# Mixer side chains resumed by an estimate of operand times instead of counted delays, on one Trainium2 core

## The chip, the core and the metric

The kernel runs on one core of one Trainium2 chip. The metric is the device time of one execution in microseconds (us). Names of engines are those of the profile: PE is TensorE's matmul queue, PEld its weight loads, DVE is VectorE, ACT is ScalarE, POOL is GpSimd, SP is SyncE, which issues nearly all DMAs here. Line numbers (L610) are those of the kernel before; where a line of the changed kernel is meant, the text says so.

## What is computed

One layer over 2048 tokens of width 1024, in fp32. The part that the change touches is the mixer:

```python
p = h @ w_in[layer]
gate_b, gate_c, h_conv, q, k, v, z, a, bt = jnp.split(p, split_at, axis=-1)
ya = gate_b * causal_depthwise_conv(gate_c * h_conv, conv_w_mix[layer])       # then a grouped rms_norm
q, k, v = silu(causal_depthwise_conv([q, k, v]))                               # q and k then L2-normalised
g_dec = -exp(a_log) * softplus(a + dt_bias)
o = chunked_gated_delta_rule(q, k, v, g_dec, beta)    # per chunk: decay matrix, triangular solve, state step
yb = rms_norm(o, g_dn_out[layer]) * silu(z)
x = x + gate_m * (concat([ya, yb]) @ w_out[layer])
```

Ahead of it stands a normalisation with modulation by `c`, behind it a gated feed-forward layer of hidden width 2816 and a final normalisation. Those are the same in both kernels.

## The kernel before

**Tiling.** The mixer works through four blocks of 512 tokens (b = 0 to 3). A block has 28 projections of 128 output columns (4 heads each of k, q, v and z, then 12 for the short convolution, in triples `cg`, `hc`, `gb`). A projection is 24 matmuls of 128x128 by 128x512: 8 slices of the inner dimension times three products of high and low halves (`whi`/`wlo` for weights, `hTh`/`hTl` for activations), since each fp32 operand is split into two fp32r parts. These are recorded by `dmm` (L122) into the PSUM tiles `pd` and are called dense matmuls below. Each strip of weights is loaded by SP, rounded on ACT (`whi`, L189) and its remainder taken on DVE (`wlo`, L191); up to three strips stand ready ahead. The block ends with the output projection, 2 x 96 dense matmuls. After the mixer comes the feed-forward part.

**Side chains.** Everything that is not a dense matmul is written as Python generators that record instructions and `yield`. `dmm` counts dense matmuls, and after each sixth it calls `tick`, which resumes every chain whose delay has run out; `yield n` means "resume after n ticks", that is after 6n dense matmuls. So the numbers behind `yield` and the delays of `spawn` decide where in each engine's instruction stream a chain's next piece stands. (The framework that records the program moves some instructions between engines' queues afterwards, so the true places are read from the built program.) All engines execute their own queue in order.

**The chains of a block, in the order in which they depend on each other:**

- `head_chain`, first part: `proj_ab` (L536) gives 16 rows per token block; they are copied, transposed (L629), and a softplus with a series is computed in small steps, 18 of them on POOL, down to `g` (L659). Then `yield 7`, three small matmuls (L670 to L672), an exponential `eg`, and per head the decay matrix `E` (L680 to L688).
- `head_chain`, second part, per head: k is transposed to tokens (L610) and scaled by `eg` into `kd` (L696); its norm `nk` (L697); k times k (L704), times `E` into `M` (L706, tile name `ym`), scaled on POOL (L707), masked on POOL (L710) and reduced on DVE into the head's part of `Dg` (L714).
- The inversion of the 32x32 diagonal blocks: `Dg` of all four heads goes to DRAM (`dm`) and comes back in another layout (`mq`, part of a tile named `yal`); then 31 steps of two DVE instructions (L736, L738) that depend on each other; the result goes to DRAM (`dx`) and comes back as `xc` (tile name `Dg`); POOL spreads it into `X` (L752, 32 instructions).
- `level_chain`, twice two heads: transposes of `X` on DVE (L768), a masked `M` called `Mm` (L770), matmuls L775 and L782, and then the half-size steps L790 to L804, which complete the inverse.
- `q_chain` (L817, L818), `v_chain` (L830), then `chunk_chain`, four chunks of 128 tokens in sequence through `state`, and per chunk `out_chain`, which gives the hi and lo halves that the output projection reads. `mix_chain` (L957 to L963) normalises the convolution branch into `yah` and `yal`.
- `second_norm` of the block before (L295 to L362) runs beside a block; its transposes are L360.

Small matmuls and transposes of all chains go to the PSUM tiles `pm`, four in rotation, so a chain's matmul can wait until an older user of its `pm` tile has been read. Scratch tiles in SBUF rotate too: `cv` (4), `lv` (6), `ch` (4).

Of the kernel before, what the change touches and what calls it, by code (L numbers as in the profile page):

```python
# [37 lines left out]
PRE = 3  # L38
HALF = 1024


def constants():
    i = np.arange(P)
    r, c = i[:, None], i[None, :]
    parts = [r == c, r <= c, r > c, r // 64 == c // 64]
    for b in LEVELS:
        parts.append((r // (2 * b) == c // (2 * b)) & (r % (2 * b) < b) & (c % (2 * b) >= b))
    parts.append(r // BASE == np.arange(NBASE)[None, :])
    return np.ascontiguousarray(np.concatenate(parts, axis=1).astype(np.float32))


@with_exitstack
def layer_kernel(ctx, tc, x, c, w_ada, b_ada, w_ada_final, b_ada_final, g_norm_mix, g_norm_ffn, g_norm_final,
# [49 lines left out]
    side, count = [], [0]  # L103
# [4 lines left out]
    def tick():  # L108
        for e in list(side):
            e[1] -= 1  # L110
            if e[1] <= 0:
                try:
                    e[1] = next(e[0]) or 1
                except StopIteration:
                    side.remove(e)

    def drain():
        while side:
            tick()
# [219 lines left out]
    def transpose_split(tiles, gcol, scol, hh, hl):  # L339
        for k in range(KD):  # L340
            scale_split(transpose_k(tiles, k), k, gcol, scol, hh, hl)
            yield 2
# [8 lines left out]
    def second_norm(b):  # L351
        for i in range(CH):
# [3 lines left out]
            yield 2  # L356
            for q in range(2):
                ps = misc_ps()
# [5 lines left out]
                yield 1  # L364
# [93 lines left out]
    with ExitStack() as actx:  # L458
# [117 lines left out]
        for b in range(NB):  # L576
            hh, hl = hT
            if b:
# [39 lines left out]
            def wait(key, n):  # L618
                while done[key] < n:
                    yield 1  # L620


            def head_chain(ps, b=b):
                abr = cv_tile([P, BLK])[:16, :]
                nc.vector.tensor_copy(abr, ps[:16, :])
                yield 1
                ps = misc_ps()
                for j in range(CH):
                    nc.tensor.transpose(ps[:, j * 16:(j + 1) * 16], abr[:, j * P:(j + 1) * P], ident[:16, :16])  # L629
                ab2 = ap_.tile([P, CH, 16], F32, name="ab2")  # L630
# [36 lines left out]
                yield 7  # L667
# [8 lines left out]
                for h in range(NH):  # L676
                    rgs = []
# [4 lines left out]
                    yield 3  # L682
                    ps = misc_ps()
                    for i, rg in enumerate(rgs):
                        mm(ps, strict_r, rg.rearrange("p j c -> p (j c)"), start=(i == 0), stop=(i == 1))
                    e = ap_.tile([P, CH, P], F32, name="E", bufs=4)
# [5 lines left out]
                for h in range(NH):  # L692
                    yield from wait("k", h + 1)
                    pk = to_tokens(kT[:, h, :])
# [13 lines left out]
                    Ms.append(M)  # L708
                    md = lv_tile([P, CH, NBASE, BASE])
# [3 lines left out]
                    yield 2  # L713
                    nc.vector.tensor_reduce(Dg[:, h], md.rearrange("p j b c -> p j c b"), op=ALU.add, axis=AX.X)  # L714
                nc.gpsimd.tensor_mul(sk, sk, nk)
                done["sk"] = True
                yield 3
# [12 lines left out]
                yield 4  # L730
                prt = lv_tile([P, CH * P])
                for k in range(BASE - 1, 0, -1):
# [6 lines left out]
                    yield 1  # L739
# [5 lines left out]
                yield 14  # L745
# [9 lines left out]
                spawn(level_chain((2, 3)), 3)  # L755


            def level_chain(hs):
# [5 lines left out]
                for lv in LEVELS:  # L764
                    T, Mm, Y = {}, {}, {}
                    for h in hs:
                        T[h] = lv_tile([P, CH, P])
                        nc.vector.transpose(T[h].rearrange("p j c -> p (j c)"), Xs[h].rearrange("p j c -> p (j c)"))  # L768
                        Mm[h] = lv_tile([P, CH, P])
                        nc.gpsimd.tensor_mul(Mm[h], Ms[h], bm(lmask[lv], CH))  # L770
                    yield 2
                    for h in hs:
                        py = misc_ps()
                        for j in range(CH):
                            mm(py[:, j * P:(j + 1) * P], Mm[h][:, j, :], T[h][:, j, :], start=True, stop=True)  # L775
                        Y[h] = lv_tile([P, CH, P])
                        nc.scalar.copy(Y[h].rearrange("p j c -> p (j c)"), py)
                    yield 2
                    for h in hs:
                        pz = misc_ps()  # L780
                        for j in range(CH):
                            mm(pz[:, j * P:(j + 1) * P], Y[h][:, j, :], Xs[h][:, j, :], start=True, stop=True)  # L782
                        nc.vector.tensor_sub(Xs[h], Xs[h], h4(pz))
                    yield 1
                T, Y = {}, {}
                yield 2
# [6 lines left out]
                yield 2  # L793
                for h in hs:
                    py = misc_ps()
                    for j in range(CH):
                        mm(py[H:, j * H:(j + 1) * H], Ms[h][:H, j, H:], T[h][:H, j, :H], start=True, stop=True)
                    Y[h] = lv_tile([P, CH, P])
                    nc.scalar.copy(Y[h][H:, :, :H], hh4(py[H:, :CH * H]))
                yield 2  # L800
                for h in hs:
                    pz = misc_ps()
                    for j in range(CH):
                        mm(pz[:H, j * H:(j + 1) * H], Y[h][H:, j, :H], Xs[h][H:, j, H:], start=True, stop=True)  # L804
                    nc.vector.tensor_scalar_mul(Xs[h][:H, :, H:], hh4(pz[:H, :CH * H]), -1.0)
# [3 lines left out]
            def q_chain():  # L809
                for h in range(NH):  # L810
                    yield from wait("q", h + 1)
                    yield from wait("kk", h + 1)
                    sumsq(to_tokens(qT[:, h, :]), nq, h)
# [12 lines left out]
            def v_chain(h, src):  # L826
                while "sk" not in done:
                    yield 1
                pv = to_tokens(src)
                nc.vector.tensor_mul(vt[:, :, h, :], h4(pv), bc(sk[:, h], P))  # L830
                done["vt"] += 1

            def chunk_chain():
# [5 lines left out]
                for j in range(CH):  # L839
                    ts = slice(j * P, (j + 1) * P)  # L840
                    e_g, e_l = eg[:, 0, j, :], eg[:, 1, j, :]
                    first = b == 0 and j == 0
                    if first:
                        R = vt[:, j]
                    else:
                        pks = misc_ps()
                        for h in range(NH):
                            mm(pks[:, hsl[h]], kT[:, h, ts], state[:, hsl[h]], start=True, stop=True)
                        R = ch_tile([P, NH, P])
                        nc.vector.tensor_mul(R, h4(pks), bc(e_g, P))  # L850
                        nc.vector.tensor_sub(R, vt[:, j], R)
                        yield 2
                    pw = misc_ps()
                    for h in range(NH):
                        mm(pw[:, hsl[h]], Xs[h][:, j, :], R[:, h, :], start=True, stop=True)
                    W = ch_tile([P, NH, P])
                    nc.vector.tensor_mul(W, h4(pw), bc(bk[:, :, j], P))
                    o = ch_tile([P, NH, P])
                    if not first:
                        pqs = misc_ps()  # L860
                        for h in range(NH):
# [690 lines left out]
```

## Time and profile before

| | us |
|---|---|
| median of 3 runs | 2530.69 (2530.58 to 2535.3) |
| the profiled execution | 2521.95 |
| its span in the trace | 2520.2 |
| start-up, before block 0's projections | 0 to 52 |
| blocks 0, 1, 2, 3 | 52 to 321, 321 to 612.5, 612.5 to 902, 902 to 1179 |
| feed-forward part and final normalisation | 1179 to 2520 |

Busy shares of the span are PE 94%, DVE 71%, ACT 40%, POOL 26%. The profile's lists give, per group of instructions, the number of instructions, busy time, the mean of one, and the idle time of the engine just before them with what ended it ("idle before <-releaser"). In a timeline, a row's first two numbers are its start and its duration. In a table of windows, the columns are the stretch, its length, busy time of PE, PEld, DVE, ACT and POOL (with the number of instructions), the clock granted to TensorE (1.00 is full), the DMA share and GB/s.

### The profile page before, as it was taken

The page shows a single profiled execution, that of the slowest core. Times are in us where ns is not written, and L with a number is a line of the kernel's source. Part 1 is how long each engine was busy: PE and PEld are TensorE (multiplying, and loading weights), DVE is VectorE, ACT ScalarE, POOL GpSimd, SP SyncE. Part 2 cuts the span into 40 slices and gives each one's busy share as a digit, 9 for nine tenths or more (in the row PEclk, how much of TensorE's full clock was granted, in tenths as well). Part 3 has the DMA queues.
Part 4 walks back from the last instruction along what each step waited for, and adds up shares of the span by engine and source line. Part 5 has one row for each costly group of instructions (what it writes and reads, how often), then busy time and mean ns, then how long its engine had stood idle before and what let it go on. Part 6 is the DMA issues. An engine that isn't in the chain of part 4 may idle for free. (4 is left out here: it accounts for less than half of the span.)

```text
span 2520.2 us, 30908 instructions
## 1 busy us (share of the span) xinstructions
PE 2364.0 (94%) x11243; PEld 1940.9 (77%) x11243; DVE 1791.8 (71%) x2598; ACT 1020.5 (40%) x1771; POOL 655.0 (26%) x800
## 2 busy tenths in 40 slices
PE   6899979999799989998999999999999999999996
PEld 4678767887678868886778888878888877887774
DVE  6887638865597738878566555876556658878898
ACT  3633445334633446336643333533333323322232
POOL 2622344223522444222000000000000036434426
PEclk9999989999899989999999999999999999999999
DMA  7352344524543344315674333654334374333332
GB/s 241 109 130 80 122 150 134 163 91 137 158 121 77 115 136 114 101 64 180 195 234 130 105 101 108 218 168 133 107 90 117 96 247 151 121 111 122 128 132 114
DMA packets 397535, 336.99 MB, mean 134 GB/s; under 512 B 39475, under 2 KB 338748, under 8 KB 397382
## 3 DMA queue, kind: packets, MB, share of 16 engines
q1 hardware_dynamic: 397126, 334.91, 43.7%
q8 instruction: 88, 1.44, 0.2%
q14 instruction: 65, 0.53, 0.1%
q10 hardware_dynamic: 256, 0.10, 0.0%
HBM read 261.55 MB, written 73.41 MB: 133 GB/s over the span
## 5 line engine op out<-in xcount | busy, mean ns | idle before, releaser
L189 ACT CAST whi<-wraw 128x1024 fp32r<-128x1024 f32 x278 | 291.5, 1050 | 485.9 <-PE pd L122 273.2
L191 DVE TENSOR_TENSOR wlo<-wraw,whi 128x1024 fp32r<-128x1024 f32 x275 | 347.5, 1264 | 142.2 <-ACT whi L189 129.1
L122 PE MATMUL pd<-hTh,whi 128*128 128x512 f32 x896 | 366.2, 409 | 1.2 <-DVE hTh L336 1.2
L122 PE MATMUL pd<-hTl,whi 128*128 128x512 f32 x896 | 357.1, 399 | 1.8 <-DVE hTl L337 1.8
L122 PE MATMUL pd<-hTh,wlo 128*128 128x512 f32 x896 | 355.9, 397 | 0.0
L1230 POOL TENSOR_TENSOR wraw<-wraw 128x1024 f32<-128x1024 f32 x2 | 5.0, 2498 | 789.2 <-DMA wraw<-in_w_down_dram 789.2
L122 PEld LDWEIGHTS pd<-hTh,whi 128*128 128x128 f32 x896 | 172.5, 193 | 36.8 <-DVE hTh L336 2.7
L122 PEld LDWEIGHTS pd<-hTh,wlo 128*128 128x128 f32 x896 | 171.8, 192 | 36.7
L122 PEld LDWEIGHTS pd<-hTl,whi 128*128 128x128 f32 x896 | 172.6, 193 | 35.2 <-DVE hTl L337 2.6
L1184 DVE TENSOR_TENSOR sg<-sg,pd 128x512 f32<-128x512 f32 x44 | 30.2, 687 | 169.9 <-PE pd L122 169.9
L1424 DVE TENSOR_TENSOR acc<-acc,pd 128x512 f32<-128x512 f32 x192 | 127.9, 679 | 30.4 <-PE pd L122 30.2
L1307 ACT CAST xh<-ra 128x640 fp32r<-128x640 f32 (+1 forms) x88 | 62.6, 719 | 194.7 <-PE pm L122 156.1
L935 DVE SCALAR_TENSOR_TENSOR cv<-cb,pcb,cv 128x512 f32<-128x512 f32 x144 | 114.6, 796 | 0.9
L1316 POOL TENSOR_TENSOR xl<-ra,xh 128x640 fp32r<-128x640 f32 (+1 forms) x40 | 66.4, 1659 | 160.5 <-ACT xh L1307 160.5
L1424 DVE TENSOR_TENSOR acc<-acc,pm 128x512 f32<-128x512 f32 x120 | 81.6, 680 | 17.5 <-PE pm L122 17.1
L122 PE MATMUL pd<-whi,ym 128*128 128x512 f32 x256 | 84.8, 402 | 1.5 <-ACT ym L901 1.5
L1353 POOL TENSOR_TENSOR wraw<-wraw 128x512 f32<-128x512 f32 x40 | 70.2, 1777 | 42.6 <-DMA wraw<-in_w_down_dram 36.5
L752 POOL TENSOR_TENSOR X<-Dg,ck 128x64 f32<-128x64 f32 x128 | 41.5, 361 | 148.8 <-DMA Dg<-dx 148.8
L122 PE MATMUL pd<-S2h,whi 128*128 128x512 f32 x176 | 69.5, 395 | 9.0 <-ACT whi L189 8.5
L1025 POOL TENSOR_TENSOR cv<-cv 128x512 f32<-128x512 f32 x32 | 46.1, 1447 | 105.7 <-DVE cv L1024 48.0
L122 PE MATMUL pd<-A22h,whi 128*128 128x512 f32 x176 | 68.7, 390 | 2.7 <-DVE sg L1184 2.7
L122 PE MATMUL pd<-S3h,t3h 128*128 128x512 f32 x176 | 68.9, 392 | 2.4 <-ACT sg L1170 2.3
(456 smaller groups left out, 6375.2 us busy)
## 6 DMA issues: line engine op xcount, KB each, us to landing
wraw<-in_w_in_dram SPq DMA_DIRECT2D x112, 512.0 KB
wraw<-in_w_gate_up_dram SPq DMA_DIRECT2D x88, 512.0 KB
ra<-act SPq DMA_DIRECT2D x80, 448.0 KB
act<-S SPq DMA_DIRECT2D x80, 256.0 KB
act<-act SPq DMA_DIRECT2D x68, 256.0 KB
wraw<-in_w_ada_dram SPq DMA_DIRECT2D x32, 512.0 KB
wraw<-in_w_out_dram SPq DMA_DIRECT2D x32, 512.0 KB
wraw<-in_w_down_dram SPq DMA_DIRECT2D x22, 512.0 KB
```

Source lines behind the costliest of these rows:

```text
L122: mm(*args, **kw)
L189: nc.scalar.copy(hi, raw)
L191: (lo_engines.popleft() if lo_engines else nc.vector).tensor_sub(lo, raw, hi.bitcast(F32))
L752: nc.gpsimd.tensor_mul(Xv[:, e, j], xc[:, e, h * CH + j].unsqueeze(1).to_broadcast([P, NBASE, HB]), bmb)
L935: nc.vector.scalar_tensor_tensor(cv, cb[:, t:t + BLK], tap[t], cv, op0=ALU.mult, op1=ALU.add)
L1025: nc.gpsimd.tensor_add(xr, xr, yo)
L1184: nc.vector.tensor_add(s5[i], s5[i], a[i])
L1230: nc.gpsimd.tensor_mul(r, r, first_w["gate"])
L1307: nc.scalar.copy(hi, raw[:, c0:c1, :])
L1316: eng.tensor_sub(lo, raw, hi.bitcast(F32))
L1353: nc.gpsimd.tensor_mul(r[:, hs], r[:, hs], gate_f[:, hs])
L1424: nc.vector.tensor_add(accs[s, u][:, ns], accs[s, u][:, ns], ps)
```

## The change

**When a chain resumes.** A chain no longer yields a number of ticks but the tiles that its next piece reads. `tick` resumes it when `due(tiles)` is not after `clock.pe`. `Clock` is a running estimate: every recorded instruction is passed to `note`, which gives each engine a start and an end by fixed costs per kind, places work of other engines than PE into the first gap that fits, and remembers per tile and offset when it was written (`written[name][offset]`). `due` is the latest of the tiles' times and of the time at which the fourth-last `pm` tile was last used, plus 0.3. `ready(ap)` looks the tile up under its own offset and, if that offset is known, returns that entry alone; only for an unknown offset does it take the latest of all. A DMA costs 1.2 to start, its bytes at 240 GB/s, and 0.9 behind.

**Places promised.** `take(tag, n)` holds a chain back until n tiles of `cv`, `lv` or `ch` are free by count, `give` returns them, `take_now` does the same for the main loop by resuming other chains. Waits for a counter poll each tick (`POLL`). `done["k"]` and `done["q"]` are counted as soon as the main loop has recorded the projection, where before a delay of 7 or 10 ticks was put in between; v's chain had a delay of 8.

**Moves.** `Mm` takes its tile from `ym` (8 in rotation) instead of `lv`. In `chunk_chain` the product of q with `state`, the scaling of `state` on POOL and `o` are recorded together with the product of k with `state`, ahead of the `X` product. The inversion yields after every second step. `transpose_split` yields ahead of a piece instead of behind it.

The core of the diff:

```diff
+    def ready(self, ap):
+        w = self.written.get(ap.name)
+        return 0.0 if not w else w[ap.offset] if ap.offset in w else max(w.values())
...
+    def due(w):
+        return max([clock.next_free("pm"), *(clock.ready(t) for t in w)]) + 0.3
+
+    def tick(must=False):
+        ran = False
         for e in list(side):
-            e[1] -= 1
-            if e[1] <= 0:
+            if isinstance(e[1], int):
+                e[1] -= 1
+                go = e[1] <= 0
+            else:
+                go = due(e[1]) <= clock.pe
+            if go:
                 try:
-                    e[1] = next(e[0]) or 1
+                    e[1] = next(e[0])
...
-                yield 7
+                yield g, g_hi, g_lo
                 ps = misc_ps()
...
-                    yield 2
+                    yield md,
                     nc.vector.tensor_reduce(Dg[:, h], md.rearrange("p j b c -> p j c b"), op=ALU.add, axis=AX.X)
...
-                yield 4
+                yield mxq,
+                yield from take("lv", 1)
                 prt = lv_tile([P, CH * P])
...
-                    yield 1
+                    if k % 2:
+                        yield mxq,
...
-                yield 14
+                yield xc,
...
-                        Mm[h] = lv_tile([P, CH, P])
+                        Mm[h] = ap_.tile([P, CH, P], F32, name="ym", bufs=8)
                         nc.gpsimd.tensor_mul(Mm[h], Ms[h], bm(lmask[lv], CH))
-                    yield 2
+                    yield *T.values(), *Mm.values()
...
-            for key, c0, dstT, wait_for in (("k", 2048, kT, 7), ("q", 1536, qT, 10), ("v", 2560, None, 8)):
+            for key, c0, dstT in (("k", 2048, kT), ("q", 1536, qT), ("v", 2560, None)):
```

**What it moves, place 1: PE at the head of block 2.** L629 (L752 in the changed kernel) transposes the 16 rows, L670 (L794) is the first matmul that needs `g`. The queue of PE before:

```order
L629 MATMUL pm<-ck,cv 128x16 x4
L122 MATMUL pd<-hTh,whi 128x512
L122 MATMUL pd<-hTl,whi 128x512
...
L670 MATMUL pm<-g,ck 128x16
L671 MATMUL pm<-g,ones_r 128x16
L672 MATMUL pm<-g,ck 128x16
```

and in the changed kernel:

```order
L752 MATMUL pm<-ck,cv 128x16 x4
L244 MATMUL pd<-hTh,whi 128x512
L244 MATMUL pd<-hTl,whi 128x512
...
L794 MATMUL pm<-g,ck 128x16
L795 MATMUL pm<-g,ones_r 128x16
L796 MATMUL pm<-g,ck 128x16
```

Between the first and the fourth of these places stand 42 dense matmuls before and 66 now (block 0: 42 and 60, block 1: 42 and 66, block 3: 42 and 72), and in blocks 1 to 3 eight transposes of `second_norm` in both.

**Place 2: PE in block 2, from the last k times k to the first level matmul.** Before, L704 of the last head is followed, 336 dense matmuls later (342, 336, 336, 342 in the four blocks), by

```order
L704 MATMUL pm<-kq 128x128 x4
...
L775 MATMUL pm<-lv 128x128 x8
L122 MATMUL pd<-hTh,whi 128x512
...
L782 MATMUL pm<-X,lv 128x128 x8
L775 MATMUL pm<-lv 128x128 x8
```

In the changed kernel there are 164 dense matmuls in between (176, 216, 164, 173), and 24 small ones of the q and v chains (one more in block 1):

```order
L831 MATMUL pm<-kq 128x128 x4
...
L909 MATMUL pm<-lv,ym 128x128 x8
L917 MATMUL pm<-X,lv 128x128 x8
L909 MATMUL pm<-lv,ym 128x128 x8
L926 MATMUL pm<-ck,X 64x64 x8
L917 MATMUL pm<-X,lv 128x128 x8
```

Counted in projections from a block's start, the last k times k stood behind 9.3, 7, 7 and 6.8 of them and now stands behind 11.3, 11.5, 11.8 and 10.8; the first level matmul stood behind 23.5, 21, 21 and 21 and now stands behind 18.6, 20.5, 18.6 and 18.

**Place 3: DVE in block 2, from the last reduction into `Dg` to the inversion.** `lv<-yal` and `yal<-yal,lv` are the inversion's two instructions, `cv<-cb,pcb,cv` are taps of the convolution, `wlo<-wraw,whi` splits a strip of weights. Before:

```order
L714 TENSOR_REDUCE Dg<-lv 128x128
...
L736 TENSOR_TENSOR lv<-yal 128x31
L935 SCALAR_TENSOR_TENSOR cv<-cb,pcb,cv 128x512
L738 TENSOR_TENSOR yal<-yal,lv 128x31
L929 COPY cb<-halo_2766 128x3
L935 SCALAR_TENSOR_TENSOR cv<-cb,pcb,cv 128x512
L736 TENSOR_TENSOR lv<-yal 128x30
```

and in the changed kernel:

```order
L842 TENSOR_REDUCE Dg<-lv 128x128
...
L972 TENSOR_TENSOR vt<-pm,sk 128x4x128
L313 TENSOR_TENSOR wlo<-wraw,whi 128x1024
L866 TENSOR_TENSOR lv<-yal 128x31
L868 TENSOR_TENSOR yal<-yal,lv 128x31
L866 TENSOR_TENSOR lv<-yal 128x30
L868 TENSOR_TENSOR yal<-yal,lv 128x30
```

The taps of the v projections stood among the inversion's steps; now they stand ahead of it, and among its 62 rows stand only splits of weight strips: four in block 2 (for the projections 15 to 18 of the block), four in block 0, five in block 1 with five rows of a background sum (L376 in the changed kernel) and some taps, four in block 3.

More of the change, by code (lines that the diff above doesn't have):

```diff
@@ L38 @@
 PRE = 3
+POLL = -1
 HALF = 1024
@@ L676, in head_chain @@
                 for h in range(NH):
+                    yield from take("lv", 2)
                     rgs = []
@@ L765, in level_chain @@
                     T, Mm, Y = {}, {}, {}
+                    yield from take("lv", len(hs))
                     for h in hs:
@@ L842, in chunk_chain @@
                     first = b == 0 and j == 0
+                    yield from take("ch", 2 if first else 3)
+                    o = ch_tile([P, NH, P])
                     if first:
@@ L949, in mix_chain @@
             def mix_chain(m, cv):
+                yield from take("cv", 1)
+                yield from take("lv", 2)
                 sy = cv_tile([P, BLK])
```

190 lines of the change are left out of this document (152 added, 38 removed).

## The prediction

> **What bounds the kernel now.** I read the page's busy times first, then a table of windows by stage, then PE's list of waits, then the places that it names in the timeline.
>
> ```profile
> PE 2364.0 (94%) x11243; PEld 1940.9 (77%) x11243; DVE 1791.8 (71%) x2598; ACT 1020.5 (40%) x1771; POOL 655.0 (26%) x800
> ```
>
> ```profile
> 52.00:321.33 269.33, 250.56 (x1319) 208.08 (x1318) 203.26 (x329) 121.10 (x244) 99.08 (x145) 0.98 0.38 107
> 321.33:612.50 291.17, 269.17 (x1428) 223.52 (x1427) 202.79 (x336) 129.32 (x257) 100.91 (x155) 0.97 0.47 135
> 612.50:902.00 289.50, 268.79 (x1412) 222.16 (x1411) 200.18 (x327) 131.33 (x260) 106.86 (x157) 0.97 0.42 120
> 902.00:1179.40 277.40, 263.07 (x1380) 217.55 (x1378) 198.24 (x328) 132.13 (x268) 93.05 (x143) 0.98 0.41 119
> 1179.40:2520.20 1340.80, 1285.58 (x5603) 1049.73 (x5603) 951.65 (x1230) 486.15 (x711) 238.59 (x174) 0.99 0.44 140
> ```
>
> PE bounds every stage. The change removes no dense matmul, so it can only move PE's idle time and its granted clock. In the four blocks PE is idle 1127.4 - 1051.6 = 75.8 us; in the feed-forward part, which is the same code, 55 us. What the idle time waits for:
>
> ```profile
> PE pm L670 <- POOL g L659: 31.4, 4, 8.8
> PE pm L360 <- ACT wraw L355: 12.2, 5, 4.2
> PE pd L122 <- ACT whi L189: 8.5, 1, 8.5
> PE pm L610 <- DVE nk L697: 6.8, 2, 3.4
> PE pm L817 <- DVE ym L706: 3.3, 2, 3.0
> PE pm L775 <- POOL lv L770: 2.8, 1, 2.8
> PE pd L122 <- ACT yah L962: 2.7, 2, 1.4
> PE pm L895 <- POOL ch L890: 2.3, 1, 2.3
> PE pm L610 <- DVE kd L696: 2.2, 1, 2.2
> PE pm L817 <- DVE kd L696: 1.6, 1, 1.6
> PE pd L122 <- ACT ym L901: 1.5, 1, 1.5
> ```
>
> One wait leads: four times, once per block, PE waits for `g`, the end of the head chain. A stall also costs clock behind it. Block 2's stall, and the windows behind those of blocks 0 and 1 and behind a shorter L360 gap:
>
> ```profile
> 620.71 0.42 PE L629 MATMUL pm<-ck,cv 16*128 16x16 f32 x4
> 630.32 0.39 PE L122 MATMUL pd<-hTh,whi 128*128 128x512 f32 x1
> ...
> 631.46 0.39 PE L122 MATMUL pd<-hTh,wlo 128*128 128x512 f32 x1
> 639.39 0.61 PE L670 MATMUL pm<-g,ck 128*128 128x16 f32 x2 [7.54 <-POOL g L659]
> ```
>
> ```profile
> 80.30:84.70 4.40, 4.39 (x13) 3.76 (x14) 0.23 (x2) 2.86 (x5) 4.30 (x6) 0.50 0.21 62
> 347.80:354.30 6.50, 6.47 (x18) 5.41 (x19) 1.85 (x3) 0.00 (x0) 6.38 (x7) 0.50 0.27 81
> 357.70:361.20 3.50, 3.37 (x12) 3.08 (x13) 0.00 (x0) 3.44 (x6) 0.00 (x0) 0.51 0.05 4
> ```
>
> Six dense matmuls start in 631.46 - 630.32 = 1.14 us, five steps: 0.228 each. At a granted clock of 0.50 half of the stretch is lost: 2.2 and 3.25 us behind two head stalls, 2.7 on the mean, 10.9 for four.
>
> **The change part by part.**
>
> *Head chain (gain 30).* PE's queue has 18, 24, 24 and 30 more dense matmuls between L629 and L670: 96 x 0.228 = 21.9 us of cover that the stalls had not. The chain itself (620.71 to 639.39 in block 2, 18.7 us on POOL and ACT) loses no instruction. 31.4 - 21.9 = 9.5 us stay, in gaps of 1 to 3.4 us. Of the 10.9 us of slow clock I leave 3, since the L360 gap shows that a short gap can bring it too. Gain 21.9 + 7.9 = 29.8. If the new cover is itself late, up to 10 of it goes.
>
> *Waits for a `pm` tile (gain 14).* L610 and L817 wait for `nk`, `kd` and `ym` because their tile's older reader on DVE is late: 6.8 + 3.3 + 2.2 + 1.6 = 13.9. `due` now asks for the fourth-last tile's last use. Two 3.4 us gaps also bring 3.5 us of half clock each (the L360 row is the nearest), 3.5 lost in both. Of 17.4 I leave 3, since the estimate is no measurement: 14. Bounds 5 and 17.
>
> *Smaller waits (gain 8).* L775, `yah`, L895 and the output projection's `ym` make 2.8 + 2.7 + 2.3 + 1.5 = 9.3. `Mm` no longer waits for an `lv` place and chunk chains end earlier in the block; 8 of it goes. The stall on `whi` (8.5, at the feed-forward's start) waits behind what ACT does for block 3's tail; that tail moves ahead: I take 6, bounds 0 and 12.
>
> *L360 (12.2):* `second_norm` waits for the same ACT and POOL rows in the changed order; the gaps only change places. Nothing, bounds -4 and 4.
>
> *The new cost: the level chain (41 + 11).* This is what the shifted delays reveal. From the last k times k to the first level matmul PE had 336 dense matmuls in block 2, 336 x 0.228 = 77 us, and the chain between them fitted in. Now it has 164: 37.4 us, and 24 small matmuls beside them (0.13 each by the L817 row below): 40.5. What must happen in that time, by rows of block 2:
>
> ```profile
> L706 DVE TENSOR_TENSOR ym<-pm,E 128x512 f32<-128x512 f32 x4 | 2.7, 678 | 0.0
> L707 POOL TENSOR_TENSOR ym<-ym,bk 128x512 f32<-128x512 f32 x4 | 5.6, 1406 | 0.3 <-DVE nk L697 0.3
> L710 POOL TENSOR_TENSOR lv<-ym,ck 128x512 f32<-128x512 f32 x4 | 4.5, 1125 | 0.2
> L714 DVE TENSOR_REDUCE Dg<-lv 128x128 f32<-128x512 f32 x4 | 4.3, 1072 | 4.8 <-POOL lv L710 4.8
> L736 DVE TENSOR_TENSOR lv<-yal 128x126 f32<-128x126 f32 (+22 forms) x31 | 7.8, 251 | 0.6
> L191 DVE TENSOR_TENSOR wlo<-wraw,whi 128x1024 fp32r<-128x1024 f32 x36 | 47.6, 1322 | 26.3 <-ACT whi L189 22.1 <-PE pm L855 2.2 <-PE pm L685 2.0
> L752 POOL TENSOR_TENSOR X<-Dg,ck 128x64 f32<-128x64 f32 x32 | 11.5, 399 | 33.8 <-DMA Dg<-dx 33.8
> L768 DVE STREAM_TRANSPOSE lv<-X 128x512 f32<-128x512 f32 x4 | 2.6, 682 | 0.0
> ```
>
> ```profile
> 702.47 1.06 PE L817 MATMUL pm<-kq 128*128 128x128 f32 x8
> 707.40 1.08 DVE L714 TENSOR_REDUCE Dg<-lv 128x128 f32<-128x512 f32 x1
> 716.91 0.19 DVE L736 TENSOR_TENSOR lv<-yal 128x31 f32<-128x31 f32 x1
> 751.88 0.18 DVE L738 TENSOR_TENSOR yal<-yal,lv 128x16 f32<-128x16 f32 x1
> 758.66 11.52 POOL L752 TENSOR_TENSOR X<-Dg,ck 128x64 f32<-128x64 f32 x32 [33.81 <-DMA Dg<-dx]
> ```
>
> Step by step:
> - L706, L707, L710, L714 back to back are 0.68 + 1.41 + 1.13 + 1.07 = 4.3 us. On DVE `kd`, a `wlo` and a product with `E` stand between; I take 6.5. In blocks 0 and 1 three rows of `Mm` (1.4 each, as L707) stand ahead on POOL as well: 10.5.
> - `Dg` out to `dm` and back as `mq`: from 708.48 to 716.91, 8.4 us.
> - The inversion: two rows of each of 31 steps, 62 x 0.251 = 15.6, and what stands among them: four `wlo`, 5.3, together 20.9 (35.1 in the trace, where the taps stood among them). Block 1 has five `wlo`, five sums of about the same length and 2.6 of taps, 31.4 in all; block 3 has 23.
> - `dx` out and back as `xc`: 752.06 to 758.66, 6.6.
> - `X` of the first two heads: 16 of 32 rows, 5.8. Two transposes, 1.4.
>
> Block 2: 6.5 + 8.4 + 20.9 + 6.6 + 5.8 + 1.4 = 49.6 against 40.5: PE waits 9.1 us. Blocks 0, 1 and 3 the same way: 53.6 - 43.3, 64.1 - 52.4, 51.7 - 42.6, that is 10.3, 11.7 and 9.1. Sum 40. The first part of each stall may show at a `wlo` behind the inversion, since DVE's queue holds the splits for projections 15 to 18 while it waits for `mq`; that divides the stall and doesn't add to it. Behind each comes the half clock of a head stall, 2.7: 11 for four. New short gaps in the level and chunk chains, where L909 and L917 now follow each other without dense matmuls between: 1 per block, 4.
>
> Why does the planner resume the chain too early? `ready` looks `Dg` up under its own offset, which is that of head 0's part, so it takes the DMA to `dm` to be possible as soon as head 0 is reduced, although the tile is whole only with head 3. The 8.4 us then lie in the past for it.
>
> *Other edits* (counts instead of delays for k and q, the moved products in `chunk_chain`, the inversion's yield) add no instruction; they are in the order that was counted.
>
> *Sum against the profiled execution:* -30 - 14 - 8 - 6 + 40 + 11 + 4 = -3, so 2521.95 - 3 = 2519. The median of the runs lies 8.7 us above that execution, so 2528. A measurement of this kernel can tell about 0.2% (5 us) from no change, and -3 is inside.
>
> The Trainium skill bears on two terms. Its page "TensorE: Matmul & The Clock Gate", section "What's actually happening", says that one idle window of about 3.4 us brings the half clock and one busy window lifts it. Here 4.4 and 6.5 us passed at 0.50, and shorter gaps brought it too, so the trace differs in size; by the page's 3.4 us each large stall would cost 1.7, removed and added alike, and the sum would be some 3 us lower. Its page "DMA: Bandwidth & Descriptors", section "Anatomy of one DMA", gives a fixed cost of about 2 us per DMA (there for GpSimd's path), mostly the receipt of the write; two in a row would be some 4 us and the bytes, by estimate 6, where the trace has 8.4 from reduction to first step; by it the level stalls would be some 10 us shorter in all.
>
> **The rivals.**
>
> *A, slower: the level stall is longer than worked out.* The chain crosses in-order queues at seven places. If in block 2 the reduction comes 10.5 instead of 6.5 us after k times k (the price in blocks 0 and 1) and steps of the inversion keep gaps that make it 23, the stall is 9.1 + 4 + 2.1 = 15. Six more in each block is 24: 2552. It decides for slower once the mean stall passes 10 + (5 + 3) / 4 = 12 us. For it: in the trace no such step met its bare sum. Against: DVE is emptier now while it runs.
>
> *B, faster: the level stall is about half.* The 8.4 us hold a wait of SP's queue behind other DMAs and of DVE for its own earlier rows; at 6 us, and 4.3 for the first step, the stall is 4.5 per block, with less slow clock: -22 in all, 2506. For it: POOL and DVE have less in their queues there. Against: blocks 0 and 1 carry the extra `Mm` rows.
>
> *C, the change doesn't do what it says:* the estimate misses DVE's true lateness, so waits for `pm` stay where they were (14 lost), with the rest as forecast: 2542.
>
> **How the numbers follow.** Forecast 0.42, A 0.25, B 0.24, C 0.09. The time is that of the forecast, 2528; its own range, from the bounds of the gains (9 for the `pm` waits, 6 for the feed-forward's start, 4 for L360, as independent errors about 12), is 2516 to 2540. The range for 8 in 10 reaches to A and B: 2502 to 2554. Below 2525.6 is faster, above 2535.8 slower. The forecast gives 0.19 to faster, 0.16 to the same and 0.07 to slower; A 0.01 to the same and 0.24 to slower; B 0.24 to faster; C 0.04 to the same and 0.05 to slower. Together 0.43, 0.21, 0.36.
>
> **What would show it.** In the changed kernel's list of PE's waits, L794 on `g` should fall from 31.4 to about 10, waits of L732 and L957 on `nk`, `kd` and `ym` to under 4, and a new wait of about 40 us should stand at L909 (on `lv`, the transposed `X`, or `X`), partly at L244 on `wlo`, in four pieces, with a granted clock near 0.5 behind each. On DVE the time from the last L842 to the first L866 should be about 8 us with little work in it. The forecast is wrong if L909 waits under 20 us (B) or over 55 (A), or if L794 still waits 25.

## The result and the profile after

The changed kernel takes 2595.9 us (median of 4 runs, 2589.46 to 2596.92) against 2531.2 us of the kernel before on the same chip: ratio 1.0247, 95% interval 1.0227 to 1.0267. It is 65 us slower, where 2528 was forecast and 2554 was the upper end of the range. The profiled execution has a span of 2594.3 us.

The table of windows of the changed kernel, with the four blocks cut at the first matmul that makes the 16 rows of the head chain, and the feed-forward part:

```profile
42.50:339.80 297.30, 267.70 (x1366) 220.73 (x1365) 215.83 (x346) 119.67 (x247) 107.17 (x151) 0.94 0.37 104
339.80:651.50 311.70, 277.59 (x1435) 230.25 (x1434) 210.16 (x336) 125.61 (x255) 93.77 (x156) 0.93 0.43 126
651.50:956.40 304.90, 275.72 (x1408) 228.30 (x1407) 203.32 (x327) 128.94 (x258) 95.25 (x156) 0.94 0.40 114
956.40:1253.00 296.60, 266.55 (x1371) 221.24 (x1370) 207.86 (x339) 137.43 (x275) 94.08 (x144) 0.94 0.39 111
1253.00:2594.30 1341.30, 1286.44 (x5609) 1049.98 (x5608) 945.37 (x1218) 482.68 (x703) 236.68 (x174) 0.99 0.44 140
```

The kernel before, cut at the same places, has

```profile
42.40:321.30 278.90, 259.14 (x1365) 214.23 (x1364) 211.69 (x345) 123.14 (x249) 100.68 (x151) 0.98 0.39 110
321.30:614.20 292.90, 270.90 (x1436) 224.82 (x1435) 202.79 (x336) 129.32 (x257) 102.64 (x156) 0.97 0.46 134
614.20:902.80 288.60, 267.89 (x1408) 221.41 (x1407) 200.18 (x327) 131.33 (x260) 105.96 (x156) 0.97 0.42 120
902.80:1179.50 276.70, 262.30 (x1377) 217.03 (x1375) 198.34 (x328) 132.24 (x268) 92.25 (x144) 0.98 0.41 119
```

The feed-forward part is the same to 1 us. All of the loss lies in the blocks: 1137.1 us became 1210.5, 73 more between the two profiled executions (the one before was 9 us faster than its median, so the medians differ by 65). PE's busy time there rose from 1060.2 to 1087.6 for nearly the same number of matmuls, with the granted clock down from 0.97 and 0.98 to 0.93 and 0.94; so 27 us are slower matmuls, and 46 are idle time (76.9 became 122.9). PE's list of waits says where the idle time stands now:

```profile
PE pm L732 <- ACT cv L1079: 32.1, 4, 11.7
PE pm L482 <- ACT wraw L477: 22.7, 6, 7.8
...
PE pm L909 <- DVE lv L901: 18.7, 4, 5.6
...
PE pm L810 <- ACT eg L798: 9.6, 2, 5.6
PE pm L1041 <- POOL ch L1035: 8.3, 5, 3.1
PE pm L794 <- POOL g L783: 7.2, 3, 6.1
PE pm L831 <- ACT ht L484: 7.0, 2, 3.5
...
PE pd L244 <- ACT whi L311: 6.1, 1, 6.1
```

The wait for `g` did fall, from 31.4 to 7.2 us, and the new wait at the level chain (L909) is there, but 18.7 and not 40. Three others had no place in the forecast: the transposes of v wait 32.1 us for ACT's silu, and the waits on `eg` (9.6) and `ht` (7.0) are new. A fourth was forecast not to change: the transposes of `second_norm` (L482, before L360) wait 22.7 us instead of 12.2.

The longest, in block 1, by the timelines of POOL, DVE, ACT and PE (start, duration, and in brackets the idle time of that engine before the row):

```profile
456.07 1.87 POOL L903 TENSOR_TENSOR ym<-ym,ck 128x512 f32<-128x512 f32 x1
...
458.09 1.26 POOL L903 TENSOR_TENSOR ym<-ym,ck 128x512 f32<-128x512 f32 x1
...
459.76 1.03 POOL L960 TENSOR_TENSOR rq<-nq,mhalf 128x4 f32<-128x4 f32 x1
460.88 0.23 POOL L961 TENSOR_SCALAR rq<-rq 128x4 f32<-128x4 f32 x1
461.19 1.04 POOL L834 TENSOR_TENSOR ym<-ym,bk 128x512 f32<-128x512 f32 x1
462.31 1.04 POOL L838 TENSOR_TENSOR lv<-ym,ck 128x512 f32<-128x512 f32 x1
```

```profile
463.38 1.04 DVE L842 TENSOR_REDUCE Dg<-lv 128x128 f32<-128x512 f32 x1 [4.81 <-POOL lv L838]
464.34 1.32 DVE L313 TENSOR_TENSOR wlo<-wraw,whi 128x1024 fp32r<-128x1024 f32 x1
...
466.16 2.32 DVE L1078 SCALAR_TENSOR_TENSOR cv<-cb,pcb,cv 128x512 f32<-128x512 f32 x3
```

```profile
468.51 0.63 ACT L1079 ACTIVATE cv<-cv 128x512 f32<-128x512 f32 x1 [9.60 <-DVE cv L1078]
```

```profile
469.20 1.12 PE L732 MATMUL pm<-ck,cv 128*128 128x128 f32 x4 [11.72 <-ACT cv L1079]
```

This is a convoy across four in-order queues. The masked `M` of the last head (L838) is late on POOL, behind rows of `Mm` (L903) and of the q chain (L960, L961). The reduction into `Dg` has already been put into DVE's queue and holds it for 4.81 us, with the taps of v behind it; ACT's silu waits for the taps, and PE's transpose of v for the silu. Nothing in it is long; each row was placed as if the one before it were done. In blocks 0, 2 and 3 PE waits 7.6, 5.8 and 7.0 us at the same place, and the reduction just ahead waits 4.0, 2.5 and 0.9 us for POOL; what else makes v late there was not followed. In the whole program DVE waited 17.1 us in front of this reduction before, and 37.4 now:

```profile
DVE Dg L714 <- POOL lv L710: 17.1, 9, 2.9
```

```profile
DVE Dg L842 <- POOL lv L838: 37.4, 14, 4.8
```

Behind the stall PE ran 6.8 us at a granted 0.55, the table of windows says:

```profile
457.50:469.20 11.70, 0.00 (x1) 0.01 (x1) 6.78 (x13) 2.10 (x4) 6.66 (x9) 0.68 0.51 116
469.20:476.00 6.80, 6.80 (x20) 5.51 (x21) 6.30 (x16) 0.43 (x1) 0.00 (x0) 0.55 0.64 166
```

### The profile page after: what moved, and what is told of

Read it like the earlier page. It is cut to its first block, busy times and chain, and to the rows that moved or that the text cites. A ratio compares the mean times of both kernels' runs of the same rounds, so it can differ in the third digit from the quotient of the medians.

```text
span 2594.3 us, 30936 instructions
## 1 busy us (share of the span) xinstructions
PE 2392.5 (92%) x11243; PEld 1964.3 (76%) x11243; DVE 1809.3 (70%) x2598; ACT 1012.7 (39%) x1765; POOL 642.7 (25%) x800
## 5 line engine op out<-in xcount | busy, mean ns | idle before, releaser
L313 DVE TENSOR_TENSOR wlo<-wraw,whi 128x1024 fp32r<-128x1024 f32 x275 | 341.9, 1244 | 124.5 <-ACT whi L311 121.1
L244 PE MATMUL pd<-hTh,whi 128*128 128x512 f32 x896 | 372.8, 417 | 1.1 <-DVE hTh L458 1.1
L244 PE MATMUL pd<-hTl,whi 128*128 128x512 f32 x896 | 363.1, 405 | 1.1 <-DVE hTl L459 1.1
L244 PE MATMUL pd<-hTh,wlo 128*128 128x512 f32 x896 | 362.6, 405 | 0.0
L1078 DVE SCALAR_TENSOR_TENSOR cv<-cb,pcb,cv 128x512 f32<-128x512 f32 x144 | 124.9, 867 | 1.9
L884 POOL TENSOR_TENSOR X<-Dg,ck 128x64 f32<-128x64 f32 x128 | 33.4, 301 | 155.2 <-DMA Dg<-dx 155.2
L244 PE MATMUL pm<-S4h,whi 128*128 128x512 f32 x176 | 68.9, 391 | 1.1 <-ACT sg L1333 1.1
```

The source lines that it names most:

```text
L244: mm(*args, **kw)
L313: (lo_engines.popleft() if lo_engines else nc.vector).tensor_sub(lo, raw, hi.bitcast(F32))
L884: nc.gpsimd.tensor_mul(Xv[:, e, j], xc[:, e, h * CH + j].unsqueeze(1).to_broadcast([P, NBASE, HB]), bmb)
L1078: nc.vector.scalar_tensor_tensor(cv, cb[:, t:t + BLK], tap[t], cv, op0=ALU.mult, op1=ALU.add)
```

## The experiments

Theory 1: the convoy on DVE's reduction is the cause. Theory 2: the DRAM round trip of `Dg` is not counted, so the level chain comes too early. Theory 3: there is no slack anywhere, so every lateness ends in a PE wait, and what is mended at one place comes back at another. Theory 4: the old stall on `g` had a second waiter in its shadow. Theories 5 and 6 came up with the runs. Times are medians, and each ratio is to the kernel before on the same chip.

**p1_reduce_late**

```diff
                     yield md,
+                    yield 2
                     nc.vector.tensor_reduce(Dg[:, h], ...)
```

> The changed kernel with one edit: after the yield on md, two more ticks (12 dense matmuls) pass before the reduction into Dg (L842) is recorded. Theory 1 (convoy on DVE): in the changed kernel that reduction stands in DVE's queue 37.4 us too early in all, ahead of the convolution taps of v; ACT's silu and then PE's transposes of v wait behind it (PE waits 32.1 us at L732 for the silu). Then the wait at L732 falls under 12 us and the time by 25 to 40 us, to 2556 to 2571. Theory 2 (the DRAM round trip of Dg is not counted, so the level chain is resumed too early: PE waits 18.7 us at L909): the L732 wait is only where this lateness shows first, L909's wait stays at 15 to 20 and the time falls by under 10 us. Theory 3 (no slack anywhere: every resume stands 0.3 us behind an estimate): what goes at L732 comes back at other places, 10 to 20 us are won.

Measured 2588.1 us, ratio to the kernel before 1.0224 (1.0207 to 1.0241), 8 us below the changed kernel. The wait of L732 for the silu is gone from the list, and the time is not:

```profile
PE pm L910 <- DVE lv L902: 36.1, 4, 14.8
PE pm L482 <- ACT wraw L477: 24.5, 7, 8.0
...
PE pm L1107 <- ACT lv L1103: 15.1, 2, 9.3
```

The level chain (L910 here) now waits 36.1 us and `mix_chain` 15.1. Theory 1 names the place rightly, but the 25 to 40 us that it forecast did not go: the lateness is waited for further on. The fall of under 10 us is theory 2's, though it had L909 stay at 15 to 20 us.

**p3_dma_whole**

```diff
+        if op == "DMACopy":
+            start = max([start, *(v for a in ins for v in self.written.get(a.name, {}).values())])
```

> The changed kernel with one edit in its Clock: a DMA is taken to be ready when the latest piece of the tile that it reads is written, not the piece at the same offset. This sets the inversion and the level chain later. Theory 2: the wait at L909 falls from 18.7 to under 5 us and with its half clock 20 to 27 us are won, 2569 to 2576. Theory 1: the wait at L732 for v stays at about 32 us, and the time falls only by what L909 gave, 10 to 20 us. Theory 3: as theory 1, or less, since waits move on.

Measured 2575.6 us, ratio 1.018 (1.0161 to 1.0198), 20 us below the changed kernel. The wait at the level chain falls from 18.7 to 2.7 us, the wait for v's silu stays at 33.3 (L734 here). Theory 2 holds for its own place, at the edge of what both theories gave it, and doesn't explain the rest.

**p5_slack4**

```diff
-        return max([clock.next_free("pm"), *(clock.ready(t) for t in w)]) + 0.3
+        return max([clock.next_free("pm"), *(clock.ready(t) for t in w)]) + 4.0
```

> The changed kernel with one number changed: every resume stands 4.0 us behind the estimate instead of 0.3. Theory 3 (too little slack in general): PE's idle time in the mixer falls from 123 us to 80 or less, the time to 2535 to 2555. Theory 1 alone: the wait at L732 falls, the others stay, 2560 to 2575. Against both: a chain has some 20 resumes, so it grows by up to 74 us, and the end of a block waits for chunk chains: no gain, 2590 or more, with waits at the output projection.

Measured 2563.9 us, ratio 1.0129 (1.0109 to 1.0149), 32 us below the changed kernel. One number, that knows nothing of any chain, is worth more than either repair. The forecast of theory 3 was 2535 to 2555, so it was too hopeful. The time lies in theory 1's range (2560 to 2575), and the wait for v falls from 32.1 to 2.7 us, as theory 1 has it; but other waits do not stay as they were: L482 falls from 22.7 to 9.4, and the transposes of `o` and `eg` rise. What stays is L909 (23.7), which theory 2 explains:

```profile
PE pm L909 <- DVE lv L901: 23.7, 4, 7.1
...
PE pm L1041 <- POOL ch L1035: 17.5, 12, 2.9
PE pm L810 <- ACT eg L798: 17.0, 2, 9.6
```

**p4_head_only**, the first term of the prediction alone, on the kernel before:

```diff
-                yield 7
+                yield 11
                 ps = misc_ps()
```

> The kernel before with one number changed: the yield ahead of the first matmul that needs g is 11 ticks instead of 7 (24 more dense matmuls, as the changed kernel has between these places). The prediction's first term: the wait of 31.4 us for g falls to about 10 and most of the 10.9 us of half clock goes: 25 to 33 us won, 2498 to 2506. Rival: the chain behind is late by as much, waits at L610, L704 and L817 take its place and under 10 us are won.

Measured 2556.7 us, ratio 1.0099 (1.0084 to 1.0114): 24 us slower. The wait for `g` fell as expected, and a larger one took its place, at the transposes of `second_norm`:

```profile
PE pm L360 <- ACT wraw L355: 48.0, 5, 16.2
...
PE pm L670 <- POOL g L659: 4.8, 1, 4.8
```

The timelines of POOL, ACT and PE in block 1 show why:

```profile
351.83 0.22 POOL L659 TENSOR_TENSOR g<-sp_p,nexpa 128x16 f32<-128x16 f32 x1
...
360.11 1.04 POOL L680 TENSOR_TENSOR lv<-ck,g_lo 128x512 fp32r<-128x512 f32 x1
361.24 0.19 POOL L301 TENSOR_SCALAR ss<-ss 128x1 f32<-128x1 f32 x1
361.51 0.57 POOL L302 TENSOR_TENSOR ss<-ss,mhalf 128x1 f32<-128x1 f32 x1
```

```profile
362.11 1.15 ACT L355 ACTIVATE wraw<-wraw,ss 128x1024 f32<-128x1024 f32 x1 [9.79 <-POOL ss L302]
```

```profile
363.31 1.97 PE L360 MATMUL pm<-ck,wraw 128*128 128x128 f32 x8 [16.18 <-ACT wraw L355]
```

`second_norm`'s scale `ss` is two small rows on POOL, and they stand behind the head chain and six rows of L680. In the kernel before the same transposes stood behind L670 and waited only 2.61 us, since PE had stood still for `g` until then:

```profile
347.82 0.61 PE L670 MATMUL pm<-g,ck 128*128 128x16 f32 x2 [8.82 <-POOL g L659]
...
357.83 1.97 PE L360 MATMUL pm<-ck,wraw 128*128 128x128 f32 x8 [2.61 <-ACT wraw L355]
```

With `g` moved back, PE reaches them first, stands for 16 us, and the new cover stands in its queue behind them. So in the kernel before the stall on `g` hid a second wait, longer than itself. (In blocks 1 to 3 of p4 sixteen of these transposes stand ahead of L670, in the kernel before eight, and ahead of L794 in the changed kernel eight as well. So p4's 24 us are not a part of the changed kernel's loss.)

**p6_head_norm_late**, p4 with `second_norm` started later, on the kernel before:

```diff
-                spawn(second_norm(b - 1), 4)
+                spawn(second_norm(b - 1), 16)
...
-                yield 7
+                yield 11
```

> The kernel before with 11 ticks instead of 7 ahead of the first matmul that needs g, as in the last head experiment, and with the normalisation of the block before started after 16 ticks instead of 4. Theory 4 (the stall on g had a second waiter in its shadow: the normalisation's small rows on POOL stand behind the head chain's, and PE holds its transposes ahead of the work that was meant as cover): the wait at L360 falls from 48.0 to under 15 us and the time from 2557 to 2505 to 2520. Rival: the transposes wait as long at their new place, 2545 to 2560.

Measured 2530.3 us, ratio 0.9997 (0.9987 to 1.0007): 26 us better than p4, and no better than the kernel before. The longest wait at L360 falls from 16.2 to 6.5 us, as theory 4 has it, but the sum only to 34.1, in 11 pieces instead of 5:

```profile
PE pm L360 <- ACT wraw L355: 34.1, 11, 6.5
```

So neither theory 4's numbers (under 15 us, 2505 to 2520) nor the rival's time came. The wait at `g` fell from 31.4 to 9.2 us and the one at L360 rose from 12.2 to 34.1: by the list it changed its place, and nothing was won.

**p7_after_norm_late**, the same delay of `second_norm` in the changed kernel:

```diff
-                spawn(second_norm(b - 1), 4)
+                spawn(second_norm(b - 1), 16)
```

> The changed kernel with one number changed: the normalisation of the block before starts after 16 ticks instead of 4. Theory 4: the wait at L482 falls from 22.7 to under 10 us, with it the waits on eg (9.6) and on ht (7.0) that stand behind the same ACT and POOL rows, and 20 to 35 us are won, 2560 to 2576. Rival (no slack, the waits move on): under 10 us won.

Measured 2576.9 us, ratio 1.0178 (1.0161 to 1.0195), 19 us won. `eg` and `ht` are off the list and v's wait halves to 15.5, but the transposes of k and q now wait 8.4 us for their silu, L482 keeps 17.0 and the wait for `g` is back at 20.3, against 7.2: between the two theories.

**p8_counts**, the changed kernel with every resume put back to the old counts:

```diff
-                yield g, g_hi, g_lo
+                yield 7
...
-                    yield md,
+                    yield 2
...
-                yield xc,
+                yield 14
...
+                        spawn(bump(key), 7 if key == "k" else 10)
```

> The changed kernel with every resume time put back to the counted delays of the kernel before (also the delays for k, q and v); the promised places, Mm in ym and the reordered products of the chunk chain stay. If the running estimate is the cause of the loss, this stands within 10 us of the kernel before, 2522 to 2542. If the other parts (places, Mm, chunk chain) carry part of the loss, it stands 15 us or more above it.

Measured 2550.9 us, ratio 1.0081 (1.0062 to 1.01), 19 us above the kernel before. So the time at which chains are resumed (the running estimate, the dropped delays of k, q and v and the moved yields, all put back here together) is worth some 45 of the 65 us, and the parts that were taken for free are worth about 20.

**p9_slack4_whole**, p3 and p5 together:

> The changed kernel with both earlier edits of the estimate: 4.0 us behind it instead of 0.3, and a DMA ready only when the whole tile is. Theories 2 and 3 together: the wait at L909 falls from 23.7 (with 4.0 alone) to under 6, and 15 to 30 us go on top of the 32 that 4.0 us alone won, 2535 to 2550. Rival: the level chain is now so late that the chunk chains hold up the output projection, 2560 or more.

Measured 2547.3 us, ratio 1.0058 (1.0039 to 1.0078): 49 us below the changed kernel; the two repairs alone gave 32 and 20, so they nearly add. The level chain's wait is 0.5 us. With p8's 19 us for the other parts still in it, the estimate with these two edits is no worse than the counts that were set by hand.

**q1_chunk_only** (the kernel before, with the chunk chain's products moved) and **q2_counts_chunk_back** (p8 with them put back) ask which of the other parts costs the 19 us:

```diff
                         pks = misc_ps()
...
+                        pqs = misc_ps()
+                        for h in range(NH):
+                            mm(pqs[:, hsl[h]], qT[:, h, ts], state[:, hsl[h]], start=True, stop=True)
                         R = ch_tile([P, NH, P])
```

> The kernel before with one part of the change: in the chunk chain the product of q with state, the scaling of state on POOL and o are recorded with the product of k with state. The counted version of the changed kernel stood 19 us above the kernel before, with 12.6 us of waits at the transposes of o on POOL's ch rows against 2.3. Theory 5a (this move puts the scaling of state, which must wait for PE, ahead of out_chain's rows on POOL): 2545 to 2555, with that wait near 12. Theory 5b (the promised places or Mm in ym carry it): 2527 to 2537.

> The counted version of the changed kernel with the chunk chain's products put back: only the promised places and Mm in ym are left of the change. Theory 5a: 2525 to 2537. Theory 5b: 2545 to 2555.

Measured 2531.4 us, ratio 0.9999 (0.9987 to 1.0011), and 2551.0 us, ratio 1.0074 (1.0059 to 1.0089). The products cost nothing by themselves: theory 5a falls, 5b stands.

**r1_mm_only** (the kernel before, with `Mm` in `ym`) and **r2_mm_back** (q2 with `Mm` in `lv` again, so that only the promised places are left):

```diff
-                        Mm[h] = lv_tile([P, CH, P])
+                        Mm[h] = ap_.tile([P, CH, P], F32, name="ym", bufs=8)
```

> The kernel before with one part of the change: Mm takes its tile from ym (8 in rotation) instead of lv. Theory 6a (a free place lets Mm's rows, 1.4 us each, move ahead on POOL, in front of the masking rows that the reduction into Dg waits for, so DVE's queue, the silu behind it and PE wait): 2543 to 2555, with DVE waiting for POOL at the reduction for about 30 us instead of 17. Theory 6b (the promised places shift the chains): 2527 to 2537.

> The counted version of the changed kernel with the chunk chain's products and Mm put back: only the promised places are left of the change. Theory 6a: 2525 to 2537. Theory 6b: 2545 to 2555.

Measured 2536.8 us, ratio 1.0026 (1.001 to 1.0042), and 2543.2 us, ratio 1.0048 (1.0033 to 1.0064), some 7 and 12 to 14 us: both carry it. (r1's time lies in theory 6b's range and r2's between the two.) For `Mm` the mechanism shows in DVE's waits in front of the reduction into `Dg`, in r1:

```profile
DVE Dg L714 <- POOL lv L710: 25.5, 12, 4.7
```

and in q2 and r2, the same program with `Mm` in `ym` and in `lv`:

```profile
DVE Dg L842 <- POOL lv L838: 26.4, 13, 4.7
```

```profile
DVE Dg L842 <- POOL lv L838: 17.1, 9, 2.9
```

With its own tiles `Mm` no longer waits for an `lv` place. Its rows move forward on POOL, in front of the masking that the reduction waits for: in block 0 three of its four rows stand ahead of the last head's L707 and L710, where all four stood behind them. A place that comes free earlier made the critical row later.

**q3_best** (p9 with the chunk chain's products put back) and **q4_best_norm** (and `second_norm` after 16 ticks):

> The changed kernel with 4.0 us behind the estimate, a DMA ready only with the whole tile, and the chunk chain's products put back. Theory 5a with theories 2 and 3: the wait at the transposes of o falls from 22.4 to under 10, 2525 to 2538. Theory 5b, or waits that move on: 2543 to 2555.

> As q3_best, and the normalisation of the block before starts after 16 ticks instead of 4. If the normalisation's rows on ACT and POOL still collide with the head chain (eg 19.3, L482 9.7 with 4.0 us alone): 8 to 20 us below q3_best. If waits only move on: within 6 us of it.

Measured 2537.4 us, ratio 1.0022 (1.0012 to 1.0032), and 2525.5 us, ratio 0.9972 (0.9957 to 0.9986). In q3 the wait at the transposes of `o` fell to 14.5 us and not under 10. The last beats the kernel before by 0.28%, and the changed kernel by 70 us. It holds one more count set by hand, the 16 ticks, and the kernel before was not run with these alone; so it does not show that the estimate beats the counts. In its list of PE's waits `g` and the level chain are no longer among the long ones. The longest single wait is now at the start of the feed-forward part, where the kernel before waited 8.5 us:

```profile
PE pd L246 <- DVE wlo L315: 14.6, 1, 14.6
...
PE pm L1044 <- POOL ch L1038: 12.6, 10, 3.7
PE pm L484 <- ACT wraw L479: 9.9, 4, 3.1
PE pm L812 <- ACT eg L800: 6.2, 2, 4.5
```

Putting the products back was worth 10 us here, where they cost nothing in q1.

**r4_best_slack6**, q4 with 6.0 instead of 4.0:

> As q4_best_norm with 6.0 us behind the estimate instead of 4.0. If lateness against the estimate is still what PE waits for, 5 to 15 us below it, 2510 to 2520. If the end of the block is already the bound, 2526 or more.

Measured 2541.4 us, ratio 1.0047 (1.0029 to 1.0064). More slack is worse again; waits appear inside the chunk chain (L1002, 14.4 us in 11 pieces, against 4.2 in q4).

## Why the prediction was wrong, point by point

The step that failed is the list of new waits. The sum has one, at the level chain (40 us, and 4 for short gaps behind it), and puts the rest at nothing or at a gain. The level wait came out at 18.7 us. Chains that had no term, or a term of nothing, brought the loss: v 32.1 us, `second_norm` 10.5 more, `eg` and `ht` 16.6, and slower matmuls 27, where the gains and costs of clock in the sum about cancel.

- **"Head chain (gain 30)" failed.** The wait for `g` fell by 24 us, as counted. But the sentence "96 x 0.228 = 21.9 us of cover that the stalls had not" took the added cover as new. These dense matmuls had stood behind `g` and covered the next links of the chain there. By the traces of blocks 1 and 2, 54 dense matmuls run between L672 and the second pair of matmuls for `E` (L685) in the kernel before, and 24 between L796 and the same pair (L810) in the changed one. PE now waits there, at `second_norm`'s transposes and for `eg`, in block 1 so:

```profile
368.55 0.40 PE L794 MATMUL pm<-g,ck 128*128 128x16 f32 x2 [0.26 <-POOL g L783]
...
374.24 0.66 PE L482 MATMUL pm<-ck,wraw 128*128 128x128 f32 x4 [2.00 <-ACT wraw L477]
...
384.14 1.19 PE L810 MATMUL pm<-lv,strict_r 128*128 128x512 f32 x2 [5.58 <-ACT eg L798]
```

  With counts instead of the estimate it is the same in the end: 24 us lost in p4, where more transposes came to stand ahead of `g`, and nothing won in p6, with the normalisation started later.
- **"L360: nothing, the gaps only change places" failed:** 12.2 became 22.7 in the changed kernel. Of that, 13.0 us stand right behind L794 (2.0, 3.2 and 7.8 in blocks 1 to 3), 3.2 ahead of it in block 3, and 6.4 at later transposes. The row L360 with its 2.61 us in block 1 stood right behind the 8.8 us stall; it was read by its own size, not by when its operand would come if the stall went.
- **"Waits for a `pm` tile (gain 14)" had the right direction**: waits on `kd`, `nk` and `ym` fall from 13.9 to 6.0 us (L417 3.0, L732 1.6, L957 1.2, L831 0.2). That is 7.9 us, within the bounds of 5 and 17 and little more than half of the size.
- **The level chain (41 + 11) had the right mechanism and the wrong cover.** In block 2 the last k times k to the first level matmul took 53.8 us (760.39 to 814.15) against 49.6 worked out. The reduction ended 11.0 us behind k times k (771.35) and not 6.5: the prediction had three rows of `Mm` ahead of the last head on POOL in blocks 0 and 1 alone, and in the trace they stand there in block 2 too (761.82 to 765.60). The inversion took 22.7 us and not 20.9; the DRAM trip was 8.1 (771.35 to 779.47) against 8.4. Even so PE waits 5.38 us there and not 9.1, since its own way to that place grew from 40.5 to 48.4 us, by the 5.8 us wait for v and the slow clock. Both waits together are 11.2 us. The reading of `ready` was right too, and p3 shows what it is worth: 20 us.
- **The missing term was v.** The order showed 16 transposes of v standing together between the k chain and the level chain, and they were counted as 0.13 us each of cover. The prediction did not ask when their silu would be ready, with the taps behind a DVE row that waits for POOL. They wait 32.1 us. With 4.0 us behind the estimate (p5) 2.7 us of that are left.
- **"Smaller waits (gain 8)" failed.** L775's went, but the wait at the transposes of `o` rose from 2.3 to 8.3, and the stall on `whi` fell by 2.4 and not 6.
- **"`Mm` no longer waits for an `lv` place" was named as a gain.** r1 shows a loss of some 7 us. The promised places, for which the prediction has no term, cost 12 (r2); the moved products, among the edits that "add no instruction", cost nothing in q1 and some 10 us beside the estimate (p9 against q3). Instructions that stay the same in number can still change their place in four queues.
- **The half clock** was set at 8 won and 11 lost. PE's busy time in the blocks rose by 27 us. Where a block had two to four stalls of 2 to 9 us, it now has four to seven of 2 to 12 us, and slow clock stands behind short ones as well: 5.7 us at 0.50 behind the 5.58 us wait for `eg`.
- **The rivals.** A, the slower one, had the sign and in block 2 both of its conditions (11.0 us to the reduction, where it has 10.5, and 22.7 for the inversion, where it has 23). Its stall of 15 us did not come, since PE was late itself. B's 4.5 us per block fit the 18.7 us measured by luck: its reason, a DRAM trip of 6 us, was not so. C fell with the waits for `pm`. A and B were both about the size of that one wait; no rival was "a wait for another chain in the same queues", though the prediction's own second row of waits (L360) was one.

What the runs settle: some 45 of the 65 us come from when chains are resumed, and 49 go when the estimate is given 4 us of slack and the whole-tile rule. What stays open: which of its rules is too early apart from that. POOL's power on 4 columns took 1.26 us (L825) where the estimate has 0.23, and engines other than PE are taken to fill gaps where their queues are in order; both are argued from the code, and neither was changed in a run. Why the promised places cost 12 us was not followed further than r2's list, where the transposes of `o` wait 10.7 us against 2.3.

## What to carry to other kernels

A stall hides every wait that would have ended during it: before counting its removal as a gain, follow each row that stands behind it in the same queue to its own operand, and ask when that would be ready if the stall were gone. Work that is moved ahead of one wait is missing behind it, where it may have covered the next one. In an in-order queue a row that is placed too early blocks all that stands behind it on its engine, so an estimate that schedules such queues needs slack of the size of its error (here 4 us instead of 0.3 was worth 32; with the other repairs in, 6 instead of 4 cost some 19). Freeing a buffer can make a kernel slower when the early row then takes its place in a queue ahead of a critical one.

## What the runs showed of the hardware

- The slow clock came behind short stalls as well. In block 2 of the changed kernel PE ran 7.1 us at a granted 1.00, stood for 3.15 us at L482, and then ran 5.7 us at 0.50:

```profile
732.30:738.00 5.70, 5.65 (x21) 4.96 (x22) 5.70 (x7) 2.96 (x4) 0.00 (x0) 0.50 0.02 3
```

  Behind the 2.00 us stall in block 1 (374.24) the next 4.3 us had 1.00.
- On POOL a power on 128 x 4 elements (L825) and a product on 128 x 512 (L834) have the same median in the changed kernel, 1.04 us over 16 rows each; the means are 1.26 and 1.08.
